# Moving weights read as two halves in turn, and the last modulation halves one chunk sooner

## Chip, cores and metric
The kernel runs on one core of one Trainium2 chip. The metric is the device time of one execution in microseconds, the median of several runs. All five engines of the core are in use: TensorE (PE; its weight loads are shown apart as PEld), VectorE (DVE), ScalarE (ACT), GpSimd (POOL) and SyncE (SP), whose queue issues nearly all loads.

## What is computed
Two transformer blocks over 256 tokens of width 2048, in float32, one after the other. Cut to its matmuls:

```python
# first block
a = rmsnorm(x);            proj = a @ w_in             # 2048 x 6662
mix = concat(hgrn2, forgetting attention, block attention)
h = x + mix @ w_out                                    # 2048 x 2048
c = rmsnorm(h)
h = h + (gelu(conv3(c @ w_gate)) * (c @ w_up)) @ w_down  # 2048 x 5632 twice, 5632 x 2048
h = h + sigmoid(rmsnorm(h) @ w_ple_gate) * (p @ w_ple_proj)
# second block
mod = silu(c_2) @ w_mod + b_mod                        # one row, 2048 x 12288: sh1 sc1 g1 sh2 sc2 g2
q, k, v, ... = (rmsnorm(x) * (1 + sc1) + sh1) @ w_in_2
x = x + g1 * (concat(window attention, latent attention) @ w_out_2)
u = relu((rmsnorm(x) * (1 + sc2) + sh2) @ w_ff1)       # 2048 x 8192
x = x + g2 * ((u * u) @ w_ff2)                         # 8192 x 2048
out = rmsnorm(x)
```

## The kernel before
Every large weight matrix is read from HBM once, in blocks of 128 partitions by 1024 float32 (two K-tiles of 512 columns, 512 KB), 757 of them. `prep` (L273 to 284) loads a block into a `raw` tile (4 buffers) and splits it: ScalarE writes `whi`, the value in float32r (L281), and VectorE writes `wlo`, the rest `raw - whi` (L282). Activations are split in the same way. A product of two float32 numbers is then three float32r matmuls: high by high, high by low, low by high.

There are two forms of the matrix product. In `linear` (L297 to 343) the activations (K-tile by 128 tokens) are the stationary operand and the weights, up to 512 columns, are the moving one. A block is 12 matmuls there: 2 halves of the tokens, 2 K-tiles, 3 products (L318 to 320). In `linear_t` (L346 to 365) 128 columns of the weights are stationary and the activations of all 256 tokens move: 24 matmuls a block (L360 to 362). `linear` does w_in, w_out, w_down, w_ple_gate, w_ple_proj, the second w_in and w_out, the first chunk of ff1 and all of ff2; `linear_t` does w_gate, w_up and ff1 chunks 1 to 15. Two small products inside the second attention (`expand`, L1287 and L1312) also have moving weights. Every matmul of `linear` and `linear_t` brings its own load of 128 stationary columns.

The host packs each matrix so that a block is one contiguous piece (`_pack`, L152). Weights are stored in their natural column order.

The order of the work is that of the program: after each block `tick()` runs what is due. A generator that is spawned yields a number of ticks after which its next part is placed, so that, for instance, a transpose is placed on TensorE's queue some blocks after its input was made. `tick()` also adds `mod_rate` to a counter and calls `mod_half()` for each whole one.

The modulation row is not made by TensorE. `mod_half()` (L910) loads half of 128 rows of the transposed w_mod (512 KB, tile `wmod`, 2 buffers), on SP's queue behind the latest weight load, and VectorE multiplies it with silu(c) and sums (L920). 192 halves make the whole row; the last 32 are done in `mlp2`, at one a tick from the end of ff1 chunk 0. `mod_upto(n)` does at once what is still missing. `mod_row` (L935) then adds the two halves and the bias (L931, L932), waits some ticks, transposes on TensorE (L940), copies on ScalarE (L942), and stores and reloads the row through HBM, so that it is on all partitions (L944, L947). The row made last is g2, which ff2 needs when it empties its accumulators (L1444).

`mlp2` runs ff1 chunks in four groups of four. After the first chunk of a group, ff2 runs on the group before: ff1 0 to 4, ff2 on 0 to 3, ff1 5 to 8, ff2 on 4 to 7, and so on. In the kernel before, `mod_upto(96)` and the g2 row come after ff1 chunk 4, right ahead of the first ff2:

```python
for g in range(4):
    for n in range(4):
        ff1(4 * g + n)
        ...
        if g == 1 and n == 0:
            self.mod_upto(96)
            self.spawn(self.mod_row([g2], 80, F))
        if n == 0 and pend is not None:
            ff2(pend, False)
```

Of the kernel before, what the change touches and what calls it, by code (L numbers as in the profile page):

```python
# [17 lines left out]
P = 128  # L18
# [3 lines left out]
CW = 512  # L22
NCH = D // CW
DFF = 5632
NF = DFF // CW
NF2 = 8192 // CW
# [122 lines left out]
    }  # L149


def _pack(w, widths, nk=2):  # L152
    k = w.shape[0]
    out = []
    c0 = 0
    for cw in widths:
        b = w[:, c0:c0 + cw].reshape(k // (nk * P), nk, P, cw).transpose(0, 2, 1, 3)
        out.append(np.ascontiguousarray(b).reshape(-1))
        c0 += cw
    return np.concatenate(out)  # L160


def layout(inputs):
    f = {k: np.asarray(v) for k, v in inputs.items()}
    sq = lambda n: f[n][0]
    x = f["x"][0]
    a = {}
    a["x"] = np.ascontiguousarray(x.reshape(2, P, D).transpose(1, 0, 2)).reshape(P, 2 * D)
    a["xT"] = np.ascontiguousarray(x.reshape(T, KT, P).transpose(2, 1, 0)).reshape(P, KT * T)
    pp = f["p"][0, 0]  # L170
    a["pT"] = np.ascontiguousarray(pp.reshape(T, 2, P).transpose(2, 1, 0)).reshape(P, 2 * T)
    a["gains"] = np.ascontiguousarray(np.concatenate(
        [f[n].reshape(c, P).T for n, c in GAINS], axis=1))
    w_in = sq("w_in")
    a["w_in"] = _pack(w_in[:, _w_in_cols()], [CW] * len(W_IN_CHUNKS))
    a["w_bf"] = np.ascontiguousarray(
        w_in[:, B_FG:B_FG + B_H].reshape(KT, P, B_H).transpose(1, 0, 2)).reshape(P, KT * B_H)
    a["w_out"] = _pack(sq("w_out"), [CW] * NCH)
    a["w_gate"] = _pack(sq("w_gate"), [CW] * NF)
    a["w_up"] = _pack(sq("w_up"), [CW] * NF)  # L180
    a["w_down"] = _pack(sq("w_down"), [CW] * NCH)
    a["w_pg"] = _pack(sq("w_ple_gate"), [CW] * NCH)
    a["w_pp"] = _pack(sq("w_ple_proj"), [CW] * NCH)
    a["w_mod"] = np.ascontiguousarray(sq("w_mod_2").T)
    a["w_in2"] = _pack(sq("w_in_2")[:, _w_in2_cols()], W_IN2_CHUNKS)
    uq = sq("w_uq_2").reshape(384, 8, 192)
    uqc = np.concatenate([uq[:, :4, :128].reshape(384, 512), uq[:, 4:, :128].reshape(384, 512),
                          uq[:, :, 128:].reshape(384, 512)], axis=1)
    a["w_uq"] = _pack(uqc, [CW] * 3, nk=3)
    ukv = sq("w_ukv_2").reshape(128, 8, 256)  # L190
    a["w_ukv"] = _pack(np.concatenate([ukv[:, :, :128].reshape(128, 1024),
                                       ukv[:, :, 128:].reshape(128, 1024)], axis=1),
                       [2 * CW] * 2, nk=1)
    a["w_out2"] = _pack(sq("w_out_2"), [CW] * NCH)
    a["w_ff1"] = _pack(sq("w_ff1_2"), [CW] * NF2)
    a["w_ff2"] = _pack(sq("w_ff2_2"), [CW] * NCH)
    a["fox_bf"] = f["fox_bf"].reshape(1, B_H)
    a["lb"] = f["lb_logits"].reshape(4, HD).T
    a["onorm"] = f["hgrn_onorm"].reshape(1, HD)
    a["c"] = f["c_2"].reshape(1, D)  # L200
    a["sinks"] = f["swa_sinks_2"].reshape(1, 16)
    a["rel"] = f["rel_bias_2"].reshape(32, 16)
    a["fing"] = f["final_norm_g_2"].reshape(1, D)
    a.update(shape_constants())
    return {k: np.ascontiguousarray(v) for k, v in a.items()}


def bc_rows(ap, n):
# [3 lines left out]
class K:  # L212
# [84 lines left out]
    def linear(self, xt, name, seq, off, cw, evac, before=None):  # L297


        nc = self.nc  # L300
# [6 lines left out]
        def products(c, b, i, w):  # L307
# [5 lines left out]
            o = ps[c][i][:, :cw]  # L313
            for j in range(2):
                xh, xl = xt(2 * b + j)
                wh = w[0][:, j * cw:(j + 1) * cw]
                wl = w[1][:, j * cw:(j + 1) * cw]
                nc.tensor.matmul(o, xh[:, sl], wh, start=st and j == 0, stop=False)  # L318
                nc.tensor.matmul(o, xh[:, sl], wl, start=False, stop=False)  # L319
                nc.tensor.matmul(o, xl[:, sl], wh, start=False, stop=en and j == 1)  # L320
# [611 lines left out]
        nc.vector.tensor_tensor(o, o, self.G("b_mod_2", k0, n), op=ALU.add)  # L932
        return o

    def mod_row(self, rows, k0, tmp):  # L935
        nc = self.nc
        col = self.mod_section(k0, 16)
        yield 2
        pt = self.aux()
        nc.tensor.transpose(pt[:16, :P], col, self.ident)  # L940
        rt = self.t(tmp, [P, 512], "t2", self.t2b)[:16, :P]
# [3 lines left out]
        n = D // len(rows)  # L945
# [174 lines left out]
    def mixer2(self, s):  # L1120
# [139 lines left out]
        def expand():  # L1260
# [18 lines left out]
            for i in range(2):  # L1279
# [3 lines left out]
                for kt in range(3):  # L1283
                    hi, lo = w2[kt]
                    xh, xl = cT[0][:, kt, sl], cT[1][:, kt, sl]
                    for l_, r_ in ((xh, hi), (xh, lo), (xl, hi)):
                        nc.tensor.matmul(pq, l_, r_, start=(k == 0), stop=(k == 8))  # L1287
                        k += 1
                do_rope(qr[i].rearrange("p (h d) -> p h d", h=8), pq.rearrange("p (h d) -> p h d", h=8), i, 8)
            yield 1  # L1290
# [15 lines left out]
            for i in range(2):  # L1306
                sl = slice(i * P, (i + 1) * P)
                for n in range(2):
                    ws = slice(n * CW, (n + 1) * CW)
                    pq = self.aux()  # L1310
                    for k, (l_, r_) in enumerate(((ch[:, sl], hi), (ch[:, sl], lo), (cl[:, sl], hi))):
                        nc.tensor.matmul(pq, l_, r_[:, ws], start=(k == 0), stop=(k == 2))  # L1312
                    nc.scalar.activation(vb[:, i, 4 * n:4 * n + 4, :].rearrange("p h d -> p (h d)"), pq, AF.Copy)
            yield 3
            for h in range(8):
# [54 lines left out]
    def out_proj2(self):  # L1370
        nc, M = self.nc, self.M
        g1 = self.g1
        self.spawn(self.mod_row(g1, 32, M))
        ss = self.t(self.C, [P, 2, 4], "ss", 2)

        def evac(c, i, ps):
# [25 lines left out]
    def mlp2(self):  # L1402
        nc = self.nc
        with ExitStack() as s:
# [64 lines left out]
            pend = None  # L1469
            for g in range(4):  # L1470
                for n in range(4):
                    ff1(4 * g + n)
                    if g == 0 and n == 0:
                        self.holdctx.close()
# [1 line left out]
                        self.mod_open(None)  # L1476
                        g2 = self.t(R, [P, D], "grow")
                        self.mod_rate = 1.0
                    if g == 1 and n == 0:
                        self.mod_upto(96)  # L1480
                        self.spawn(self.mod_row([g2], 80, F))
                    if n == 0 and pend is not None:
                        ff2(pend, False)
                pend = list(range(4 * g, 4 * g + 4))
# [30 lines left out]
```

## Time and profile before

| | us |
|---|---|
| median of 3 runs | 2290.66 (2286.03 to 2298.77) |
| the profiled execution | 2293.44 |
| its span, first to last instruction | 2291.7 |
| TensorE busy | 2246.7 |
| VectorE busy | 1573.5 |
| ScalarE busy | 1105.6 |

The mean granted TensorE clock is 0.993 of full speed. In the span's order of time: w_in, the first attention and w_out (to 467.8 us), w_gate and w_up with w_down in three groups (to 1201.8), the gate of the per-layer input and the head of the second w_in (to 1324.7), the rest of the second attention and w_out_2 (to 1548.4), ff1 and ff2 (to the end). DMA moves 226 GB/s on average. Matmuls are pipelined, so a row's duration overlaps with the next; the spacing of two starts is the pace.

### The profile page before, as it was taken

How to read it: one execution, taken by the hardware profiler on the slowest of the kernel's cores; microseconds unless marked ns; L12 is line 12 of the kernel's file. 1: busy time of each engine (PE TensorE's matmuls, PEld its weight loads, DVE VectorE, ACT ScalarE, POOL GpSimd, SP SyncE). 2: the span in 40 equal slices, each digit the busy share in tenths (PEclk: the TensorE clock that was granted, in tenths of full speed). 3: DMA queues.
4: the chain of work that ended last, by engine and by line, in shares of the span. 5: the costliest groups of instructions: out<-in, count | busy, mean ns of one | idle time of the engine just before them, and what ended most of it. 6: DMA issues, size and time to landing. Idle time of an engine off the chain costs nothing.

```text
span 2291.7 us, 34932 instructions
## 1 busy us (share of the span) xinstructions
PE 2246.7 (98%) x13714; PEld 1996.9 (87%) x13714; DVE 1573.5 (69%) x2329; ACT 1105.6 (48%) x1560; POOL 25.8 (1%) x35
## 2 busy tenths in 40 slices
PE   9999999999999999999999999999999999999998
PEld 7787887899998999989987788888878998998986
DVE  6777766777876677767777866768766555555555
ACT  6655554454444444434445655655433443443444
POOL 0000000000000000000000000000000000000000
PEclk9999999999999999999999999999999999999999
DMA  8665566677777777777778643566886566656554
GB/s 300 229 211 193 205 230 208 241 254 259 265 264 261 265 252 254 256 258 264 249 255 301 241 161 117 173 194 212 309 290 193 190 187 193 190 187 193 190 188 154
DMA packets 147537, 517.82 MB, mean 226 GB/s; under 512 B 17115, under 2 KB 21292, under 8 KB 146860
## 3 DMA queue, kind: packets, MB, share of 16 engines
q1 hardware_dynamic: 147228, 515.58, 66.3%
q8 instruction: 107, 1.75, 0.3%
q14 instruction: 58, 0.48, 0.1%
q10 hardware_dynamic: 144, 0.01, 0.0%
HBM read 513.38 MB, written 2.14 MB: 225 GB/s over the span
## 4 chain that ended last, share of the span: by engine, by line
PE 80%; DMA 7%; issue 6%; DVE 5%; ACT 1%; POOL 1%; SPq 0%; DVEq 0%; ACTq 0%; POOLq 0%
PE mm L320 14%; PE mm L319 14%; PE mm L318 14%; PE mm L362 11%; PE mm L361 11%; PE mm L360 11%; DMA wmod<-in_w_mod 6%; DVE wlo L282 2%; PE aux L382 1%; DVE wmod L920 1%; PE aux L750 1%; ACT whi L281 1%; DMA raw<-in_w_ff 0%; PE aux L824 0%; PE aux L1273 0%
## 5 line engine op out<-in xcount | busy, mean ns | idle before, releaser
L281 ACT ACTIVATE whi<-raw 128x1024 fp32r<-128x1024 f32 (+1 forms) x746 | 785.9, 1055 | 999.0 <-PE mm L320 539.9
L282 DVE TENSOR_TENSOR wlo<-raw,whi 128x1024 fp32r<-128x1024 f32 (+1 forms) x746 | 905.5, 1216 | 503.6 <-ACT whi L281 501.9
L362 PE MATMUL mm<-xt,wlo 128*128 128x256 f32 x2368 | 662.6, 280 | 5.8 <-DVE wlo L282 5.8
L361 PE MATMUL mm<-xt,whi 128*128 128x256 f32 x2368 | 661.5, 279 | 0.0
L360 PE MATMUL mm<-xt,whi 128*128 128x256 f32 x2368 | 661.5, 279 | 0.0
L361 PEld LDWEIGHTS mm<-xt,whi 128*128 128x128 f32 x2368 | 451.0, 190 | 0.3
L362 PEld LDWEIGHTS mm<-xt,wlo 128*128 128x128 f32 x2368 | 444.6, 188 | 7.4 <-DVE wlo L282 7.2
L360 PEld LDWEIGHTS mm<-xt,whi 128*128 128x128 f32 x2368 | 444.6, 188 | 0.3
L319 PE MATMUL mm<-wlo,hid 128*128 128x512 f32 x848 | 331.4, 391 | 1.0 <-DVE wlo L282 1.0
L318 PE MATMUL mm<-whi,hid 128*128 128x512 f32 x848 | 331.6, 391 | 0.0
L320 PE MATMUL mm<-whi,hid 128*128 128x512 f32 x848 | 331.2, 391 | 0.0
L920 DVE SCALAR_TENSOR_TENSOR wmod<-wmod,cact 128x1024 f32<-128x1024 f32 x192 | 234.5, 1221 | 109.3 <-DMA wmod<-in_w_mod 108.5
L318 PE MATMUL mm<-whi,xt 128*128 128x512 f32 (+2 forms) x660 | 260.3, 395 | 0.9 <-ACT whi L281 0.9
L319 PE MATMUL mm<-wlo,xt 128*128 128x512 f32 (+2 forms) x660 | 256.9, 389 | 3.5 <-DVE wlo L282 3.5
L320 PE MATMUL mm<-whi,xt 128*128 128x512 f32 (+2 forms) x660 | 256.3, 389 | 0.0
L319 PEld LDWEIGHTS mm<-wlo,hid 128*128 128x128 f32 x848 | 159.9, 189 | 35.1 <-DVE wlo L282 2.3
L318 PEld LDWEIGHTS mm<-whi,hid 128*128 128x128 f32 x848 | 159.9, 189 | 33.0
L320 PEld LDWEIGHTS mm<-whi,hid 128*128 128x128 f32 x848 | 159.8, 188 | 33.1
L319 PEld LDWEIGHTS mm<-wlo,xt 128*128 128x128 f32 x660 | 124.5, 189 | 29.3 <-DVE wlo L282 6.6
L318 PEld LDWEIGHTS mm<-whi,xt 128*128 128x128 f32 x660 | 124.3, 188 | 24.6 <-ACT whi L281 1.6
L320 PEld LDWEIGHTS mm<-whi,xt 128*128 128x128 f32 x660 | 124.4, 188 | 23.7
L318 PE MATMUL mm<-whi,mix 128*128 128x512 f32 x244 | 97.9, 403 | 0.0
(349 smaller groups left out, 1796.6 us busy)
## 6 DMA issues: line engine op xcount, KB each, us to landing
raw<-in_w_ff SPq DMA_DIRECT2D x256, 512.0 KB, 3.7
wmod<-in_w_mod SPq DMA_DIRECT2D x192, 512.0 KB, 5.0
raw<-in_w_in SPq DMA_DIRECT2D x120, 512.0 KB, 4.1
raw<-in_w_gate SPq DMA_DIRECT2D x88, 512.0 KB, 3.8
raw<-in_w_up SPq DMA_DIRECT2D x88, 512.0 KB, 4.2
raw<-in_w_down SPq DMA_DIRECT2D x88, 512.0 KB, 4.0
raw<-in_w_out SPq DMA_DIRECT2D x64, 512.0 KB, 3.8
raw<-in_w_pg SPq DMA_DIRECT2D x32, 512.0 KB, 4.6
```

What stands on the lines that cost most here:

```text
L281: nc.scalar.activation(hi[:, :ncol], raw[:, :ncol], AF.Copy)
L282: nc.vector.tensor_tensor(lo[:, :ncol], raw[:, :ncol], hi[:, :ncol].bitcast(F32), op=ALU.subtract)
L318: nc.tensor.matmul(o, xh[:, sl], wh, start=st and j == 0, stop=False)
L319: nc.tensor.matmul(o, xh[:, sl], wl, start=False, stop=False)
L320: nc.tensor.matmul(o, xl[:, sl], wh, start=False, stop=en and j == 1)
L360: nc.tensor.matmul(o, hi[:, ws], xh, start=first, stop=False, skip_group_check=True)
L361: nc.tensor.matmul(o, hi[:, ws], xl, start=False, stop=False, skip_group_check=True)
L362: nc.tensor.matmul(o, lo[:, ws], xh, start=False, stop=(b == last and j == 1), skip_group_check=True)
L382: self.nc.tensor.transpose(pt[:, j * P:(j + 1) * P], src[:, j * P:(j + 1) * P], self.ident)
L750: nc.tensor.transpose(pt[:, jo * P:(jo + 1) * P], L[:, j * P:(j + 1) * P], self.ident)
L920: nc.vector.scalar_tensor_tensor(raw, raw, 1.0, self.cact[:, us], op0=ALU.mult, op1=ALU.mult, accum_out=self.macc[:, j, u:u + 1])
```

## The change
Three edits.

The packing. Each chunk of columns of a weight matrix that is a moving operand is stored with its even columns first and its odd columns behind them. Chunks that serve as stationary operand (`turn`) keep their order. The value part of w_ukv, 1024 columns, keeps its place and size and is permuted within each of its two runs of 512.

The reading. `moving(w)` turns a slice of 2n columns into the pattern (n, 2): column 0 of the first half, column 0 of the second, column 1 of the first, and so on. TensorE thus reads the columns in their natural order from two places half a chunk apart (1024 bytes for 512 columns), and writes its output as before. Stationary operands, the splits and the loads are as they were.

The modulation. `mod_upto(96)` and the g2 row stand ahead of ff1 chunk 4, and the row's transpose is placed 5 ticks later instead of 2. The other use of `mod_row` keeps 2.

```diff
-def _pack(w, widths, nk=2):
+def _pack(w, widths, nk=2, turn=()):
...
-    for cw in widths:
-        b = w[:, c0:c0 + cw].reshape(k // (nk * P), nk, P, cw).transpose(0, 2, 1, 3)
+    for n, cw in enumerate(widths):
+        b = w[:, c0:c0 + cw]
+        if n not in turn:
+            b = np.concatenate([b[:, 0::2], b[:, 1::2]], axis=1)
+        b = b.reshape(k // (nk * P), nk, P, cw).transpose(0, 2, 1, 3)
...
-    a["w_gate"] = _pack(sq("w_gate"), [CW] * NF)
-    a["w_up"] = _pack(sq("w_up"), [CW] * NF)
+    a["w_gate"] = _pack(sq("w_gate"), [CW] * NF, turn=range(NF))
+    a["w_up"] = _pack(sq("w_up"), [CW] * NF, turn=range(NF))
...
-    a["w_ff1"] = _pack(sq("w_ff1_2"), [CW] * NF2)
+    a["w_ff1"] = _pack(sq("w_ff1_2"), [CW] * NF2, turn=range(1, NF2))
...
+def moving(w):
+    return w.rearrange("p (a b) -> p b a", a=2)
...
-                wh = w[0][:, j * cw:(j + 1) * cw]
-                wl = w[1][:, j * cw:(j + 1) * cw]
+                wh = moving(w[0][:, j * cw:(j + 1) * cw])
+                wl = moving(w[1][:, j * cw:(j + 1) * cw])
...
-    def mod_row(self, rows, k0, tmp):
+    def mod_row(self, rows, k0, tmp, wait):
...
-        yield 2
+        yield wait
...
                 for n in range(4):
+                    if g == 1 and n == 0:
+                        self.mod_upto(96)
+                        self.spawn(self.mod_row([g2], 80, F, 5))
                     ff1(4 * g + n)
...
-                    if g == 1 and n == 0:
-                        self.mod_upto(96)
-                        self.spawn(self.mod_row([g2], 80, F))
                     if n == 0 and pend is not None:
```

## Rows read from the trace of the kernel before

**Rows 1.** The page, busy time of each engine: us (share of the span) xinstructions.
```profile
PE 2246.7 (98%) x13714; PEld 1996.9 (87%) x13714; DVE 1573.5 (69%) x2329; ACT 1105.6 (48%) x1560; POOL 25.8 (1%) x35
```

**Rows 2.** Groups by form: instruction, tiles, shape, count, busy us, mean ns, idle before.
```profile
L282 DVE TENSOR_TENSOR wlo<-raw,whi 128x1024 fp32r<-128x1024 f32 x727 | 887.3, 1223 | 492.4 <-ACT whi L281 490.7
L362 PE MATMUL mm<-xt,wlo 128*128 128x256 f32 x2368 | 662.6, 280 | 5.8 <-DVE wlo L282 5.8
```

**Rows 3.** Timeline of PE (start us, duration us), ff2: matmuls 1 and 54.
```profile
2099.79 0.39 PE L318 MATMUL mm<-whi,hid 128*128 128x512 f32 x1
...
2111.80 0.39 PE L320 MATMUL mm<-whi,hid 128*128 128x512 f32 x1
```

**Rows 4.** Timeline of PE, 384-wide chunk: matmuls 1 and 8.
```profile
1423.83 0.33 PE L318 MATMUL mm<-whi,xt 128*128 128x384 f32 x1
...
1425.04 0.33 PE L319 MATMUL mm<-wlo,xt 128*128 128x384 f32 x1
```

**Rows 5.** Timeline of PE, bf16 warm-up: its last three matmuls.
```profile
4.98 0.38 PE L492 MATMUL aux<-junk 128*128 128x512 bf16 x1
5.20 0.38 PE L492 MATMUL aux<-junk 128*128 128x512 bf16 x1
5.41 0.38 PE L492 MATMUL aux<-junk 128*128 128x512 bf16 x1
```

**Rows 6.** Timeline of PE, first w_in block: two neighbours.
```profile
9.12 0.63 PE L318 MATMUL mm<-whi,xt 128*128 128x512 f32 x1
9.55 0.63 PE L319 MATMUL mm<-wlo,xt 128*128 128x512 f32 x1
```

**Rows 7.** Timeline of PE, latent attention, plain float32: two neighbours.
```profile
1425.39 0.38 PE L1254 MATMUL aux<-PT,vb 128*128 128x256 f32 x1
1425.61 0.38 PE L1254 MATMUL aux<-PT,vb 128*128 128x256 f32 x1
```

**Rows 8.** Timeline of PE, L1287: matmuls 2 and 17 of 18.
```profile
1360.13 0.40 PE L1287 MATMUL aux<-wlo,cT 128*128 128x512 f32 x1
...
1363.63 0.39 PE L1287 MATMUL aux<-wlo,cT 128*128 128x512 f32 x1
```

**Rows 9.** Timeline of PE, linear_t in w_gate: matmuls 1 and 55.
```profile
499.79 0.28 PE L362 MATMUL mm<-xt,wlo 128*128 128x256 f32 x1
...
505.91 0.28 PE L362 MATMUL mm<-xt,wlo 128*128 128x256 f32 x1
```

**Rows 10.** Windows: length, busy us (x) by engine, granted clock, DMA share, GB/s.
```profile
4.98:5.63 0.65, 0.65 (x4) 0.20 (x2) 0.04 (x1) 0.57 (x2) 0.00 (x0) 1.00 1.13 403
8.70:9.90 1.20, 1.20 (x4) 0.99 (x3) 1.20 (x3) 0.52 (x1) 0.00 (x0) 0.50 1.07 393
...
40.00:467.80 427.80, 415.15 (x1991) 343.29 (x1991) 308.78 (x582) 228.16 (x415) 17.28 (x19) 0.99 0.63 219
...
775.30:956.10 180.80, 180.80 (x1536) 180.77 (x1535) 135.12 (x175) 82.76 (x90) 0.00 (x0) 1.00 0.73 255
...
1214.50:1324.70 110.20, 106.12 (x473) 84.76 (x472) 86.44 (x125) 61.36 (x87) 2.52 (x4) 1.00 0.72 253
...
1579.10:1676.30 97.20, 91.38 (x776) 89.53 (x775) 75.80 (x99) 42.20 (x48) 0.00 (x0) 1.00 0.88 307
1676.50:1771.70 95.20, 90.62 (x386) 73.41 (x385) 57.29 (x66) 35.64 (x36) 0.00 (x0) 0.96 0.71 237
```

**Rows 11.** Timeline of PE, first ff2: around the transpose of the g2 row.
```profile
1698.48 0.40 PE L320 MATMUL mm<-whi,hid 128*128 128x512 f32 x1
1702.50 0.38 PE L940 MATMUL aux<-ident,modT 128*16 128x128 f32 x1 [3.62 <-DVE modT L932]
...
1703.96 0.63 PE L318 MATMUL mm<-whi,hid 128*128 128x512 f32 x1
...
1707.80 0.57 PE L318 MATMUL mm<-whi,hid 128*128 128x512 f32 x1
```

**Rows 12.** Timeline of DVE, first ff2: the last half.
```profile
1700.80 1.23 DVE L920 SCALAR_TENSOR_TENSOR wmod<-wmod,cact 128x1024 f32<-128x1024 f32 x1 [2.27 <-DMA wmod<-in_w_mod]
```

More of the change, by code (lines that the diff above doesn't have):

```diff
@@ L188, in layout @@
                           uq[:, :, 128:].reshape(384, 512)], axis=1)
-    a["w_uq"] = _pack(uqc, [CW] * 3, nk=3)
+    a["w_uq"] = _pack(uqc, [CW] * 3, nk=3, turn=(0, 1))
     ukv = sq("w_ukv_2").reshape(128, 8, 256)
-    a["w_ukv"] = _pack(np.concatenate([ukv[:, :, :128].reshape(128, 1024),
-                                       ukv[:, :, 128:].reshape(128, 1024)], axis=1),
-                       [2 * CW] * 2, nk=1)
+    a["w_ukv"] = np.concatenate([_pack(ukv[:, :, :128].reshape(128, 1024), [2 * CW], nk=1, turn=(0,)),
+                                 _pack(np.concatenate(np.split(ukv[:, :, 128:].reshape(128, 1024), 2, axis=1)),
+                                       [CW])])
     a["w_out2"] = _pack(sq("w_out_2"), [CW] * NCH)
-    a["w_ff1"] = _pack(sq("w_ff1_2"), [CW] * NF2)
+    a["w_ff1"] = _pack(sq("w_ff1_2"), [CW] * NF2, turn=range(1, NF2))
     a["w_ff2"] = _pack(sq("w_ff2_2"), [CW] * NCH)
@@ L1286, in expand @@
                     for l_, r_ in ((xh, hi), (xh, lo), (xl, hi)):
-                        nc.tensor.matmul(pq, l_, r_, start=(k == 0), stop=(k == 8))
+                        nc.tensor.matmul(pq, l_, moving(r_), start=(k == 0), stop=(k == 8))
                         k += 1
@@ L1311, in expand @@
                     for k, (l_, r_) in enumerate(((ch[:, sl], hi), (ch[:, sl], lo), (cl[:, sl], hi))):
-                        nc.tensor.matmul(pq, l_, r_[:, ws], start=(k == 0), stop=(k == 2))
+                        nc.tensor.matmul(pq, l_, moving(r_[:, ws]), start=(k == 0), stop=(k == 2))
                     nc.scalar.activation(vb[:, i, 4 * n:4 * n + 4, :].rearrange("p h d -> p (h d)"), pq, AF.Copy)
@@ L1372, in out_proj2 @@
         g1 = self.g1
-        self.spawn(self.mod_row(g1, 32, M))
+        self.spawn(self.mod_row(g1, 32, M, 2))
         ss = self.t(self.C, [P, 2, 4], "ss", 2)
```

## The prediction
> **What bounds the kernel now.** I read the busy line first: TensorE is busy 98% of 2291.7 us [rows 1]. That share does not say how close the stream is to its best, so I read the groups by form next [rows 2], and then the spacing of single matmuls in the timeline, start to start. The program gives the counts: a 512-wide chunk of K = 2048 is 8 blocks of 2 K-tiles, each with 2 token halves and 3 products, 12 matmuls a block. Blocks that go through linear at width 512: 13 w_in chunks (104), out_proj1 (32), w_down (88), w_pp (4), w_pg (32), two w_in2 chunks (16), out_proj2 (32), ff1 chunk 0 (8), ff2 (128): 444 blocks, 5328 matmuls. One w_in2 chunk is 448 wide and one 384 wide: 96 matmuls each. linear_t has 7104 matmuls of 256 columns (three lines of 2368 [rows 2]).
>
> In ff2, 53 steps take 2111.80 - 2099.79 = 12.01 us: 226.6 ns for 512 columns [rows 3]. At 2.4 GHz 512 columns are 213.3 ns, so 13.3 ns, 32 cycles, are not columns. Four readings say what kind of thing that is.
> - At 384 columns 7 steps take 1.21 us, 173 ns against 160: again 13 ns, though the stream is a quarter shorter [rows 4].
> - The bf16 warm-up matmuls, also 512 wide and at granted clock 1.00, stand 0.21 to 0.22 us apart [rows 5, 10]. I take 216 ns, the figure between the two.
> - The same float32r product at granted clock 0.50 takes 0.43 us a step; 512 columns at 1.2 GHz are 426.7 ns, no excess [rows 6, 10].
> - Plain float32, 256 columns in 0.22 us, is two cycles a column, with 2 to 3 ns over [rows 7].
>
> So the excess appears only where 4 bytes per partition are read in each 2.4 GHz cycle, and is per matmul (that is, per 128-column weight load) rather than per column. It also moves with place and phase: L1287, whose stationary operand is another tile, needs (1363.63 - 1360.13) / 15 = 233 ns for 512 columns [rows 8]; the 256-column stream of linear_t runs at 6.12 us / 54 = 113.3 ns in one stretch [rows 9] and at 180.8 us / 1536 = 117.7 ns in another, with the same operands [rows 10]. I read it as two SBUF reads, the moving stream and the weight load behind it, meeting now and then; order of addresses can alter that.
>
> **The change part by part.** *Two halves in turn.* No instruction, byte or DMA is added: the packing is on the host, split writes the same tiles, output columns arrive in their old order. What changes is the address of each successive moving column: neighbours become words half a chunk apart, and each half advances one word per two cycles. No row of the trace has a moving operand read this way. Bounds from rows: 216 ns from below (the bf16 stream of the same width at the same clock, [rows 5]), two cycles a column, 427 ns, from above (the plain float32 stream, [rows 7]; it reads in order, but is the slowest warm stream there is). I take 216, the end that the present 226.6 lies nearest to: three of four stream kinds have no more than that floor, and the fourth has an excess that shifts with address and phase.
>
> The sum: 5328 x (226.7 - 216) = 57.0 us; 96 x (173 - 163) + 96 x about 13 (taken as the 384 chunk's excess) = 2.2 us. Together 59.2 us if every nanosecond reaches the end. Where it does not:
> - First stages to 467.8 us: 1632 matmuls, 17.4 us. TensorE idles 12.65 us of 427.8 there [rows 10], the attention chains and the start behind loads; a shorter stream uncovers more of that. I keep 80%: -3.5.
> - w_pg with its prefetch: 384 matmuls, 4.1 us; TensorE busy 106.1 of 110.2 from 1214.5 to 1324.7 [rows 10]. I keep half: -2.1.
> - Second attention (w_in2, out_proj2), 2.0 + 2.2 + 4.1 = 8.3 us: I keep 85%: -1.3.
> - First ff2 group, 384 matmuls, 4.1 us, still behind loads at its head: -1.1.
> - w_down and the later ff2 groups: kept whole. A block would last 12 x 216 = 2.59 us, and DVE needs 1.22 us per block for wlo [rows 2], ACT less.
> That leaves 51 us. If the cover were gone everywhere but in w_down and ff2 (1056 + 1536 matmuls, less 1.1 us), 27 us would be left.
>
> [...]
>
> *linear_t* keeps its order (its chunks are excluded from the packing), so its 7104 matmuls cost what they did, unless the phase in which they start changes (a rival).
>
> *Last modulation halves.* mod_upto(96) now stands ahead of ff1(4). By the ticks 24 of the last 32 halves are due by then; so 8 halves, each a 512 KB load on SP and a DVE product of 1.23 us [rows 12] with its accumulator read, go ahead of that chunk instead of beside its 8 blocks, and with them two small DVE adds, the transpose on PE, a copy on ACT, and the store and broadcast load on SP, past ff1(4)'s 8 weight loads. The transpose comes 5 ticks later instead of 2. Now it stands some 22 us into ff2 (begun at 1676.5) and stalls the queue: 1698.48 to 1702.50, 3.8 us beyond a step, and what is queued behind it, the matmuls of ff2, then runs at half clock to 1707.80, about 12 x 0.2 = 2.5 us more [rows 11]. The whole group takes 95.2 us against 384 x 0.2267 = 87.0: 8.2 us to be had [rows 10]. Against it: ff1(1) to ff1(4), 97.2 us for 768 x 0.1133 = 87.0, already waits for loads at DMA share 0.88 and 307 GB/s [rows 10]. A 0.52 MB load costs 1.7 us at that rate, and some four halves that land in ff2 today would have to land inside this stage: +6.8 us, and the wmod tile has only two buffers. The queue order is not shown, so the ends are -8 and +8; I take -2.
>
> Total -53 us. From the profiled execution's 2293.4 us that gives 2240.4; the median of the runs shown is 2.8 us below that execution, so 2238 us.
>
> **Rivals.**
> - *linear_t locks into its shorter spacing.* Five groups, 1536 + 768 + 768 + 768 + 576 = 4416 matmuls, run at 117.7 ns (the row is of the first), all entered from linear; conv_ffn's first group runs at 113.3. A linear of another spacing may hand over in the other phase. 4416 x 4.4 = 19.5 us more: 2218 us. For it: same operands, two spacings [rows 9, 10]. Against: nothing in linear_t is edited.
> - *Half the excess goes*, or half of the gain drowns in waits: 26 + 2 us, 2263 us. For it: 233 and 226.6 ns show that the excess has levels, not just presence.
> - *Order does not matter.* The weight load still takes its 13 ns: only the -2 us are left, 2289 us. For it: the excess is the same at 384 and 512 columns. [...]
> - *Slower: each column starts a new read.* If what SBUF hands over at once serves several neighbouring columns, an order that leaves the place at every column needs a read per column. Place: every linear block. Price: up to 5328 x 200 = 1066 us, about 3355 us; at L1287's spacing 5328 x 6.6 = 35 us, about 2324. It decides from 229.2 ns a step on (13.5 us / 5328 = 2.5 ns over today). For it: in-order streams are all that the trace has. Against: excess already varies without any change of order.
> [...]
>
> **How the numbers follow.** Forecast 0.42, shorter linear_t 0.20, half 0.15, no effect 0.09, slower 0.14. A measurement of this kernel can tell about 0.5%, 11.5 us, from no change; so faster 0.77, same 0.09, slower 0.14. The forecast's own range is 2224 (all 59 us kept, modulation -8) to 2272 (cover gone, 27 us, modulation +8). The range for 8 in 10 reaches from the sum of all gains, 2290.7 - 59 - 8 - 19.5 = 2204, to no effect with a little on top, 2292; the slower case stays out.
>
> **What would show it.** In ff2 and w_down the spacing of L318 to L320: 216 ns right, 226.7 no effect, anything above 229 the slower rival. linear_t at 117.7 or 113.3 in 775 to 956. The 448 and 384 chunks by the same 10 ns or so. The transpose L940's counterpart with no 4 us gap before it and no stretch at clock 0.50; if instead waits of PE for wlo grow in ff1(4), the moved halves cost what they gave. The prediction is wrong if linear's spacing is right and the time is not below 2265, for then the cover was misjudged.

## The result, and the profile after

| | before | after |
|---|---|---|
| median, us | 2290.44 (2286.03 to 2298.77) | 2238.05 (2235.57 to 2238.65) |
| span of the profiled execution, us | 2291.7 | 2236.4 |
| TensorE busy, us | 2246.7 | 2172.8 |

The ratio is 0.9765 with a 95% interval of 0.9736 to 0.9794. The forecast said 2238. That the number is met to the microsecond is luck: the gain in `linear` came out some 8 us smaller than forecast, and `linear_t`, put at nothing, gave some 15 us. Lines have moved by 10: L318 to L320 are now L328 to L330, L360 to L362 are L370 to L372, L282 is L292, L920 is L930, L932 is L942, L940 is L950.

The page's busy line after (columns as in [rows 1]; the granted clock is 0.993, as before):

```profile
PE 2172.8 (97%) x13714; PEld 1986.3 (89%) x13714; DVE 1569.8 (70%) x2329; ACT 1104.9 (49%) x1560; POOL 25.8 (1%) x35
```

The same 13714 matmuls, 73.9 us less of them, and a share that fell from 98% to 97%: part of what the stream gave back turned into idle time. PE's timeline in ff2, two matmuls 53 steps apart (start us, duration us; the counterpart of [rows 3]), then two of the 384-wide chunk, 7 steps apart ([rows 4]):

```profile
1839.86 0.38 PE L328 MATMUL mm<-whi,hid 128*128 128x512 f32 x1
...
1851.30 0.38 PE L330 MATMUL mm<-whi,hid 128*128 128x512 f32 x1
...
1385.06 0.33 PE L329 MATMUL mm<-wlo,xt 128*128 128x384 f32 x1
...
1386.20 0.33 PE L330 MATMUL mm<-whi,xt 128*128 128x384 f32 x1
```

11.44 us over 53 is 215.8 ns where it was 226.6; 1.14 over 7 is 163 where it was 173. What a column takes, two widths read in turn show: e5 (below) has 215.8 ns for 512 columns and 135.8 for 320, so 192 columns take 80.0 ns, 0.4167 ns each, the pace that the prediction writes as a column a cycle at 2.4 GHz. A cycle below stands for these 0.4167 ns. 512 columns are then 213.3 ns and 384 are 160.0, and the excess over them fell from 13.3 ns to 2.5 and from 13 to 3. Now linear_t, which was not edited: two matmuls 54 steps apart in w_gate's second group, and behind those the windows of after (columns as in [rows 10]).

```profile
769.78 0.28 PE L371 MATMUL mm<-xt,whi 128*128 128x256 f32 x1
...
775.90 0.28 PE L371 MATMUL mm<-xt,whi 128*128 128x256 f32 x1
```
```profile
40.00:455.60 415.60, 398.59 (x1987) 343.21 (x1986) 307.24 (x580) 226.97 (x414) 17.28 (x19) 0.99 0.65 225
...
760.10:934.60 174.50, 174.42 (x1538) 174.20 (x1537) 136.00 (x177) 83.05 (x90) 0.00 (x0) 1.00 0.75 264
1183.90:1304.00 120.10, 111.85 (x516) 94.74 (x516) 90.22 (x130) 65.08 (x94) 2.54 (x4) 0.99 0.71 247
1541.90:1641.50 99.60, 91.74 (x777) 89.17 (x776) 75.93 (x98) 41.82 (x47) 0.00 (x0) 1.00 0.87 300
1641.50:1735.20 93.70, 86.11 (x387) 73.19 (x386) 57.98 (x66) 36.11 (x37) 0.00 (x0) 0.98 0.72 241
1735.30:1822.40 87.10, 87.10 (x770) 87.08 (x769) 49.01 (x49) 41.04 (x45) 0.00 (x0) 1.00 0.61 195
1905.30:1995.70 90.40, 90.40 (x769) 90.40 (x768) 49.02 (x49) 40.87 (x45) 0.00 (x0) 1.00 0.60 189
```

6.12 us over 54 is 113.3 ns; the same group took 117.7 before (180.80 us for 1536 in [rows 10], 174.50 now). Read the last two windows side by side: the same code on the same shapes, 768 matmuls each, one at 113.4 and one at 117.7. Four of the five groups that ran at 117.7 have the short spacing after the change, one (1905.3) has not.

Stage by stage, before to after, in us of span (one profiled execution each; stages cut at the first matmul of each product):

| stage | before | after | difference |
|---|---|---|---|
| w_in, first attention, w_out | 461.1 | 448.9 | -12.2 |
| w_gate and w_up, three groups | 220.5 + 180.9 + 90.5 | 221.6 + 174.5 + 87.1 | -8.7 |
| w_down (and w_pp), three groups | 87.0 + 87.1 + 80.7 | 82.9 + 83.9 + 78.3 | -9.7 |
| w_pg and the head of w_in_2 | 119.9 | 120.1 | +0.2 |
| second attention, w_out_2, ff1 chunk 0 | | | -6.8 |
| ff1 chunks 1 to 4 | 97.4 | 99.6 | +2.2 |
| first ff2 | 95.4 | 93.8 | -1.6 |
| ff1 chunks 5 to 15, three groups | 90.5 + 90.4 + 67.8 | 87.1 + 90.4 + 65.3 | -5.9 |
| ff2, other groups, and the end | 87.1 + 87.1 + 96.9 | 82.9 + 82.9 + 92.5 | -12.8 |
| all | 2291.7 | 2236.4 | -55.3 |

Not every row of this table repeats. The programs of the experiments run the same code in some stages. With linear in order (before, e2, e3, e5, e6) the first stage took 451.0 to 461.2 us and w_pg 119.9 to 123.2; with linear in turn (after, e1, e4) they took 443.4 to 448.9 and 120.0 to 121.3. On the means the first stage thus gains 9 us and w_pg 1. In the four of the in-order programs that also leave the halves alone, ff1 chunks 1 to 4 took 97.4 to 99.7 and the first ff2 93.4 to 96.0. The groups of ff1 chunks 5 to 15 and the later ff2 repeat to 0.1 us where the spacing is the same.

Last, the transpose of the g2 row in the first ff2, in PE's timeline (the counterpart of [rows 11]):

```profile
1665.68 0.38 PE L330 MATMUL mm<-whi,hid 128*128 128x512 f32 x1
1670.06 0.28 PE L950 MATMUL aux<-ident,modT 128*16 128x128 f32 x1 [4.00 <-DVE modT L942]
...
1671.47 0.63 PE L329 MATMUL mm<-wlo,hid 128*128 128x512 f32 x1
```

The stall is still there (4.00 us of waiting, 3.62 before), 28.6 us into ff2 where it was 26.0, and so is the stretch at half clock behind it (granted clock 0.50 from 1671.5 to 1674.0 us, 0.43 us a step). The modulation edit did not move what it was meant to move.

### The profile page after: what moved, and what is told of

It is laid out like the page before. It is cut to its first block, busy times and chain, and to the rows that moved or that the text cites. A ratio compares the mean times of both kernels' runs of the same rounds, so it can differ in the third digit from the quotient of the medians.

```text
span 2236.4 us, 34936 instructions
## 1 busy us (share of the span) xinstructions
PE 2172.8 (97%) x13714; PEld 1986.3 (89%) x13714; DVE 1569.8 (70%) x2329; ACT 1104.9 (49%) x1560; POOL 25.8 (1%) x35
## 4 chain that ended last, share of the span: by engine, by line
PE 73%; DMA 11%; DVE 7%; issue 6%; ACT 2%; POOL 1%; SPq 0%; DVEq 0%; POOLq 0%; ACTq 0%
PE mm L330 12%; PE mm L329 12%; PE mm L328 12%; PE mm L372 11%; PE mm L371 11%; PE mm L370 11%; DMA wmod<-in_w_mod 9%; DVE wlo L292 4%; DVE wmod L930 1%; PE aux L392 1%; ACT whi L291 1%; PE aux L760 1%; DMA raw<-in_w_ff 0%; SPq L288 0%; PE aux L1283 0%
## 5 line engine op out<-in xcount | busy, mean ns | idle before, releaser
L292 DVE TENSOR_TENSOR wlo<-raw,whi 128x1024 fp32r<-128x1024 f32 (+1 forms) x746 | 903.8, 1216 | 410.2 <-ACT whi L291 408.9
L372 PE MATMUL mm<-xt,wlo 128*128 128x256 f32 x2368 | 656.6, 277 | 6.6 <-DVE wlo L292 6.6
L370 PE MATMUL mm<-xt,whi 128*128 128x256 f32 x2368 | 655.2, 277 | 0.0
L372 PEld LDWEIGHTS mm<-xt,wlo 128*128 128x128 f32 x2368 | 444.5, 188 | 9.1 <-DVE wlo L292 8.8
L370 PEld LDWEIGHTS mm<-xt,whi 128*128 128x128 f32 x2368 | 445.7, 188 | 0.2
L930 DVE SCALAR_TENSOR_TENSOR wmod<-wmod,cact 128x1024 f32<-128x1024 f32 x192 | 234.8, 1223 | 156.2 <-DMA wmod<-in_w_mod 155.5
L329 PE MATMUL mm<-wlo,hid 128*128 128x512 f32 x848 | 322.7, 381 | 4.1 <-DVE wlo L292 4.0
L328 PE MATMUL mm<-whi,hid 128*128 128x512 f32 x848 | 322.4, 380 | 0.0
L330 PE MATMUL mm<-whi,hid 128*128 128x512 f32 x848 | 322.4, 380 | 0.0
L329 PE MATMUL mm<-wlo,xt 128*128 128x512 f32 (+2 forms) x660 | 250.8, 380 | 6.2 <-DVE wlo L292 6.0
L328 PE MATMUL mm<-whi,xt 128*128 128x512 f32 (+2 forms) x660 | 253.3, 385 | 0.9 <-ACT whi L291 0.9
L330 PE MATMUL mm<-whi,xt 128*128 128x512 f32 (+2 forms) x660 | 249.3, 378 | 0.0
L328 PEld LDWEIGHTS mm<-whi,hid 128*128 128x128 f32 x848 | 160.7, 190 | 22.6
L330 PEld LDWEIGHTS mm<-whi,hid 128*128 128x128 f32 x848 | 160.6, 189 | 22.7
L328 PEld LDWEIGHTS mm<-whi,xt 128*128 128x128 f32 x660 | 125.2, 190 | 17.4 <-ACT whi L291 1.7
L330 PEld LDWEIGHTS mm<-whi,xt 128*128 128x128 f32 x660 | 125.3, 190 | 15.5
L329 PE MATMUL mm<-wlo,mix 128*128 128x512 f32 x244 | 93.1, 382 | 2.3 <-DVE wlo L292 2.3
```

The lines of the kernel that those rows point to most:

```text
L292: nc.vector.tensor_tensor(lo[:, :ncol], raw[:, :ncol], hi[:, :ncol].bitcast(F32), op=ALU.subtract)
L370: nc.tensor.matmul(o, hi[:, ws], xh, start=first, stop=False, skip_group_check=True)
L372: nc.tensor.matmul(o, lo[:, ws], xh, start=False, stop=(b == last and j == 1), skip_group_check=True)
L930: nc.vector.scalar_tensor_tensor(raw, raw, 1.0, self.cact[:, us], op0=ALU.mult, op1=ALU.mult, accum_out=self.macc[:, j, u:u + 1])
```

## The experiments

| run | median us (lowest to highest, runs) | ratio to before, 95% interval |
|---|---|---|
| e1_order_only | 2245.14 (2239.97 to 2248.19, 5) | 0.9803, 0.9778 to 0.9829 |
| e2_halves_only | 2290.80 (2283.76 to 2298.60, 12) | 0.9999, 0.9982 to 1.0016 |
| e4_tokens_in_turn | 2222.37 (2214.86 to 2224.12, 4) | 0.9699, 0.9672 to 0.9725 |
| e7_early_halves | 2227.71 (2221.06 to 2232.05, 4) | 0.9721, 0.9696 to 0.9746 |
| e8_turn_and_early | 2210.75 (2208.15 to 2217.81, 5) | 0.9652, 0.9628 to 0.9677 |
| e9_all_halves_early | 2209.68 (2198.04 to 2215.99, 6) | 0.9625, 0.9592 to 0.9658 |

The kernel before had medians of 2287.99, 2288.76 and 2296.49 beside them (e1 to e4, e5 to e8, e9). e3, e5 and e6 were run once, for their traces.

**The two halves of the change apart.** e1 is the kernel after with the modulation edit taken back:

```diff
-                    if g == 1 and n == 0:
-                        self.mod_upto(96)
-                        self.spawn(self.mod_row([g2], 80, F, 5))
                     ff1(4 * g + n)
...
+                    if g == 1 and n == 0:
+                        self.mod_upto(96)
+                        self.spawn(self.mod_row([g2], 80, F, 2))
```

> The reading in turn alone: packing and moving() as changed, the modulation halves back behind ff1 chunk 4 with 2 ticks. Theory (the order of the moving reads is the whole gain, the moved halves give nothing): linear at 215.8 ns a step as in the changed kernel, and a time within 6 us of its 2238. Rival 1 (the moved halves cost what ff1(1..4) and the first ff2 lost, 2.2 + 2.5 us): about 2233. Rival 2 (the moved halves give 2 us or more): 2240 to 2246. linear_t may start its groups at either spacing in any kernel; each group of 768 at the other spacing is 3.4 us.

e2 is the kernel before with that edit alone.

> The moved halves alone: kernel before with mod_upto(96) and the g2 row ahead of ff1 chunk 4 and 5 ticks, weights in their old order. Theory: the order on SP, PE and POOL comes out as before, so the same stall of 4 us before the g2 transpose and the same time, 2290 +- 5; linear at 226.7 ns a step. Rival 1 (the prediction's -2 to -8): 2282 to 2288 and a gap before the transpose under 1 us. Rival 2 (halves crowd ff1(1..4)): 2295.

Measured: e1 has linear at 215.8 ns everywhere and 2245.1 us, e2 has it at 226.7 ns and 2290.8. The edit of the modulation gives nothing that shows by itself (its interval reaches from 4 us less to 4 us more, so 2 us either way can't be told), and the order is the gain. The time of e1 alone misses its theory by 1 us and lies in rival 2's range, 7 us above the kernel after; the two intervals overlap a little. In the traces it isn't the halves that cost e1 its time: its first ff2 was shorter than that of the kernel after, 89.9 us against 93.8, and what was longer is its first w_gate group, which nothing in either edit touches, 229.7 us against 221.7, most of it at 117.7 ns. The wait before the transpose goes with neither edit: 3.6 us before, 4.0 after, 2.8 in e1, 2.5 in e2.

**Why the edit of the halves does nothing.** The last 32 halves on DVE, in both kernels (count, duration in ns, then first and last start), before and after:

```profile
L920 DVE SCALAR_TENSOR_TENSOR wmod<-wmod,cact x32: 1211/1225/1226, 1579.8 to 1700.8; 128x1024 f32<-128x1024 f32 x32
```
```profile
L930 DVE SCALAR_TENSOR_TENSOR wmod<-wmod,cact x32: 1214/1225/1229, 1544.0 to 1668.4; 128x1024 f32<-128x1024 f32 x32
...
  DMA wmod<-in_w_mod: 33.2, 27
```

They take 121.0 us before and 124.4 after, one in about 4 us, and in the kernel after DVE waited for the transfer of 27 of the 32 (last line: us in all, times). Asking for eight of them a chunk sooner leaves the two `wmod` buffers and the loads behind the same weight loads as before: the rows of SP, PE and POOL stand in one and the same order in both programs.

**What the order does.** e3 is the kernel before with 48 matmuls of each of 16 forms at its end, which differ in how the moving tile is read:

```diff
+forms = [("pOrder", 512, P, same), ("pTurn", 512, P, turn(2)), ("pQuarter", 512, P, turn(4)), ...
+         ("pPair", 512, P, runs(2)), ("pStepB", 512, P, step(2)), ... ("pHalfSt", 512, 64, same), ...
+         ("pShort", 256, P, same), ("pShortTurn", 256, P, turn(2)), ("pTiny", 128, P, same), ...
```

> Kernel before with 768 extra matmuls behind its end, 48 of each form, float32r, with the activations' and weights' tile shapes of linear; the result is untouched. Steps in ns. In order 512 columns: 226.7; two halves in turn: 216. Theory A (the moving stream collides with the weight load because it walks through addresses twice as fast as the load; in turn both walk alike): quarters and eighths in turn walk slower than the load and collide again, over 216; pairs of columns in turn walk alike: 216; every second column walks four times as fast: over 216; a stationary operand of 64 or 32 columns in order: excess 1/2 and 1/4 of 10.9 ns, so about 221 and 218.5; 256 columns in order 113.3 or 117.7, in turn 109. [...]

PE's timeline of it, for each form two matmuls 30 steps apart:

```profile
2291.20 0.39 PE L519 MATMUL pOrder<-pmv,pst 128*128 128x512 f32 x1
2298.03 0.39 PE L519 MATMUL pOrder<-pmv,pst 128*128 128x512 f32 x1
...
2302.07 0.38 PE L519 MATMUL pTurn<-pmv,pst 128*128 128x512 f32 x1
2308.55 0.38 PE L519 MATMUL pTurn<-pmv,pst 128*128 128x512 f32 x1
...
2312.61 0.45 PE L519 MATMUL pQuarter<-pmv,pst 128*128 128x512 f32 x1
2321.11 0.45 PE L519 MATMUL pQuarter<-pmv,pst 128*128 128x512 f32 x1
...
2349.73 0.51 PE L519 MATMUL pPair<-pmv,pst 128*128 128x512 f32 x1
2359.58 0.51 PE L519 MATMUL pPair<-pmv,pst 128*128 128x512 f32 x1
...
2377.87 0.63 PE L519 MATMUL pStepB<-pmv,pst 128*128 128x512 f32 x1
2391.40 0.63 PE L519 MATMUL pStepB<-pmv,pst 128*128 128x512 f32 x1
...
2441.71 0.39 PE L519 MATMUL pHalfSt<-pmv,pst 128*64 128x512 f32 x1
2448.61 0.39 PE L519 MATMUL pHalfSt<-pmv,pst 128*64 128x512 f32 x1
```

In order 6.83 / 30 = 228 ns here (227 over the whole form), halves in turn 216. In the other forms quarters in turn take 283, eighths 487, two columns of each half in turn 328, every second column 451, every fourth 461, every eighth 431. Four columns of each half in turn take 246 to 254. So it is not true that any order other than the plain one escapes the excess: nearly all are worse, up to 487 ns, 0.95 ns a column. The reading that a weight load behind the matmul collides with the stream (theory A) is not borne out either: a load of 64 stationary columns instead of 128 (pHalfSt) leaves 230 ns and one of 32 leaves 232, where it asked for about 221 and 218.5, and pairs take 328 where it asked for 216. At 256 columns the plain order needs 120 ns, again 13 ns over the 106.7 of its columns, and turn 111.7; and 128 columns take 111.7 in either order, so about 111.7 ns is the least a float32r matmul with 128 stationary columns took here.

e5 varies the two streams: how far apart they are, how long each run is before the next pair of runs, where the tile starts, and bfloat16.

```diff
+("pApart257", 512, even, streams(2, 256, 257)), ... ("pApart512", 512, even, streams(2, 256, 512)),
+("pBlock128", 512, even, blocks(128)), ... ("pBlock4", 512, even, blocks(4)),
+("pFourFar", 512, even, streams(4, 128, 256)), ("pFourOff", 512, even, streams(4, 128, 132)),
+("pWide448", 448, even, order(448)), ... ("pBfOrder", ...), ("pBfTurn", halves), ("pBfStep", evens)
```

> The kernel before with extra matmuls at its end whose results are not used, 36 of each form, all with a 128-wide stationary tile unless said; only their steps are read. The earlier probe gave 226.7 ns in order and 215.8 in two halves in turn at 512 columns, 119.9 in order at 256: an excess of 32 cycles of 2.4 GHz (13.3 ns) over one column a cycle at both widths. Theory F, a fixed excess of each matmul that is read in order: pWide448 200 ns and pWide320 146.7 ns. Theory G, an excess with each so many columns: 198 and 141.7. Distance of the two streams (pApartN: columns apart, pTurn is 256): theory D1, any two streams that are far apart are free, all of pApart257 to pApart512 at 215.8; theory D2, the distance must be a multiple of 1 KB: pApart512 215.8 and the others between 226.7 and 328 (the pairs in turn of the earlier probe). pBlockN (two neighbouring runs of N columns in turn, then the next two): theory D1 215.8 down to some width and towards 328 below it (pBlock4 at 250 or more); theory D2 all of them 226.7 or worse. pFourFar and pFourOff (four streams, 256 and 132 columns apart; 128 apart gave 283): if four streams are too many 283 in both, if it was their distance 216 in one of them. pStStep (stationary tile every second column, moving in order): if the stationary tile's own read matters, other than 226.7; pStTurn with the moving tile in turn 215.8. pBfOrder, pBfTurn, pBfStep (bfloat16): no excess to take away, 213 to 216 in the first two; no number for the step.

PE's timeline of it: streams 257 columns apart, runs of 4, and four streams, each as two matmuls 30 steps apart:

```profile
2327.68 0.38 PE L535 MATMUL pApart<-pmv,pst 128*128 128x512 f32 x1
2334.15 0.38 PE L535 MATMUL pApart<-pmv,pst 128*128 128x512 f32 x1
...
2436.27 0.38 PE L537 MATMUL pBlock<-pmv,pst 128*128 128x512 f32 x1
2442.74 0.38 PE L537 MATMUL pBlock<-pmv,pst 128*128 128x512 f32 x1
...
2454.88 0.44 PE L536 MATMUL pFourOff<-pmv,pst 128*128 128x512 f32 x1
2463.04 0.44 PE L536 MATMUL pFourOff<-pmv,pst 128*128 128x512 f32 x1
```

The distance does not matter here: two streams 257, 260, 264, 272, 288, 320, 384 or 512 columns apart all stand at 215.8 ns (258 at 216.6), and runs of 128, 64, 32, 16, 8 and 4 columns too, where the two streams are 16 bytes apart. Theory D1 held further down than it claimed, D2 fell. Four streams are too many at any distance tried (283 and 272). What is shown is narrow: strictly one column of each of two streams, in turn, runs at 215.8; plain order, more streams and longer runs of each do not. In plain order the excess came in several sizes: 320 columns 146.7 ns (32 cycles over, as theory F has it), 448 columns 206.6 (48 cycles, which neither theory has), 512 columns from a start 2 columns on 233.3 (48), from 4 columns on 231.7. In turn nothing of that is seen: 189.1 ns at 448 columns and 135.8 at 320. A stationary tile that takes every second column makes 233.3 in order, where the same stream has 227.7 with the plain tile (pAgain), and 215.8 in turn, so how the stationary operand lies does have a part in the plain order's excess, though not by the width that theory A went by. Why two in turn are free is not settled by these runs.

bfloat16 behaves the other way round, against the expectation (three groups of 36, start and length; the granted clock was 1.00 in all):

```profile
2512.37 7.94 PE L544 MATMUL pBfOrder<-junk 128*128 128x512 bf16 x36
2520.15 17.60 PE L544 MATMUL pBfTurn<-junk 128*128 128x512 bf16 x36
2537.59 8.29 PE L544 MATMUL pBfStep<-junk 128*128 128x512 bf16 x36
```

From start to start, in order 7.78 / 36 = 216 ns, halves in turn 17.44 / 36 = 484, every second column 226 by its own steps.

**linear_t's two spacings.** e4 is the kernel after with the tokens, linear_t's moving operand, read in turn as well; the accumulators then hold its tokens in another order, and what empties them puts them back:

```diff
                     xh, xl = xt(2 * b + j)
+                    xh, xl = moving(xh), moving(xl)
...
-                    evac(m // 2, ps[m // 2].rearrange("p (j t) -> p j t", j=2))
+                    evac(m // 2, ps[m // 2].rearrange("p (j u i) -> p j i u", j=2, i=2))
```

> The changed kernel, and linear_t too reads its moving operand in turn: the two halves of the tokens, one token of each; its accumulators then hold the tokens in that order and are read back with stride 2 when emptied. Theory A (collision of the moving stream with the weight load, 16 to 27 cycles in 256 columns): 109 ns a step in all linear_t groups in place of 113.3 or 117.7; (1920 + 3648) x 4.3 + 768 x 8.7 = 31 us less, and nothing in ff1 chunks 1 to 4, which wait for loads: about 2207. Rival 1 (a floor of 16 cycles per 256 columns that order does not touch): 113.3 in all groups, about 2235. Rival 2 (emptying with stride 2 is slower and shows): 2240 or more, with VectorE's and ScalarE's operations on the accumulators longer than 0.68 and 0.59 us.

PE's timeline of it, 54 steps apart in w_gate's second group:

```profile
799.76 0.28 PE L377 MATMUL mm<-xt,whi 128*128 128x256 f32 x1
...
805.79 0.28 PE L377 MATMUL mm<-xt,whi 128*128 128x256 f32 x1
```

6.03 / 54 = 111.7 ns, the least of the probe, in this and every other group: between theory A's 109 and rival 1's 113.3. 2222.4 us: 0.9699 of before, 15.7 us under the kernel after by the medians, and the intervals are apart. Rival 2 is out: VectorE's and ScalarE's operations that empty the accumulators kept their 0.68 and 0.59 us.

e6 asks what chooses between 113.3 and 117.7 where the tokens are read in order:

```diff
+        if name != "w_up" and off // (D * CW) in (5, 9, 13):
+            nc.tensor.matmul(self.aux()[:, :P], xt(0)[0][:, :P], xt(0)[0][:, P:], start=True, stop=True)
```

> The kernel before with one matmul of 128 columns more (its result is not used) at the start of linear_t's chunks 5 and 9 of w_gate and 5, 9 and 13 of w_ff1, nothing else. Theory P (a phase taken at the hand-over from the 512-wide steps and kept until the next stall sets linear_t's spacing): with another matmul between them the groups of w_gate at 775 us and 1043 us and of w_ff1 at 1772, 1950 and 2127 us, all at 117.8 ns in the kernel before, change in some or all cases to 113.3; each that changes saves 4.4 ns a matmul (768: 3.4 us, 1536: 6.8 us), five of them about 19 us. Rival Q (the spacing belongs to what the group reads and where its tiles lie): all stay at 117.8, time within 3 us of before.

PE's timeline where the group begins, with the matmul put in (L353):

```profile
765.29 0.22 PE L353 MATMUL aux<-xt 128*128 128x128 f32 x1
...
765.52 0.28 PE L363 MATMUL mm<-xt,whi 128*128 128x256 f32 x1
...
771.41 0.28 PE L362 MATMUL mm<-xt,whi 128*128 128x256 f32 x1
```

The last two rows are 50 steps apart, 117.8 ns. All five groups stayed at 117.8 to 117.9, 2286.4 us: no support for theory P from this disturbance. Rival Q does not hold either, because the spacing of one and the same group differs between programs: the third w_gate group has 113.3 after and 117.8 in e7, and the first has 113.3 before and after and mostly 117.7 in e1 and e2. That first group shows more, because it changes inside one program. PE's timeline of it in e1, two matmuls 48 steps apart, then a wait, then two matmuls 48 steps apart:

```profile
458.88 0.28 PE L370 MATMUL mm<-xt,whi 128*128 128x256 f32 x1
...
464.32 0.28 PE L370 MATMUL mm<-xt,whi 128*128 128x256 f32 x1
...
465.89 0.67 PE L969 MATMUL aux<-t,ones 128*128 128x256 f32 x2 [0.60 <-DVE t L967]
...
466.63 0.28 PE L370 MATMUL mm<-xt,whi 128*128 128x256 f32 x1
...
472.28 0.28 PE L370 MATMUL mm<-xt,whi 128*128 128x256 f32 x1
```

5.44 / 48 is 113.3 ns ahead of the wait, 5.65 / 48 is 117.7 behind it, and so it stays to the end of the group. The kernels before and after have a wait in the same place and keep 113.3 behind it. In ff1 chunks 1 to 4, which wait often, the spacing changes both ways, and in the eight traces with linear_t in order it never changes within a stretch without a wait (a step of over 125 ns), a stretch's first few steps aside. So the half of theory P that says a spacing is kept until the next stall holds. The link to linear's pace shows in the counts: the five groups that the prediction's rival names had 117.8 in all five programs with linear in order, 25 of 25, and in the three with linear in turn (after, e1, e7) in 4 of 15 cases. What picks the spacing at a given stall stays open; that reading in turn ends the choice is shown.

**Where w_pg's gain went.** The waits of PE in w_pg's stage, before and after (us in total, times, longest):

```profile
PE aux L382 <- DVE hn L1101: 2.4, 1, 2.4
PE mm L319 <- DVE wlo L282: 1.4, 2, 1.1
```
```profile
PE aux L392 <- DVE hn L1111: 5.2, 2, 4.1
PE mm L329 <- DVE wlo L292: 3.0, 4, 1.7
```

3.8 us became 8.2, about the 4.1 us that the shorter stream gave there. All are on VectorE, which in the kernel after is busy 90.22 us of the 120.10. At 0.36 a step, the last 18 of the first 160 modulation halves (the expectation below counts 17) are done in a bunch, about 4 us apart, at the end of the first block, 15 of them in this stage, and the kernel before has the same bunch there. e7 issues them a little sooner, all the way from the start:

```diff
-                    self.mod_rate = 0.36
+                    self.mod_rate = 0.41
```

> The kernel after with the modulation halves issued a little faster from the first stage on (0.41 a step in place of 0.36), so that the 17 halves that were bunched at the end of the first block, 15 of them in w_pg's stage, are done before it. Theory V (w_pg's gain was eaten by VectorE, which does 15 halves of 1.3 us there beside the splitting of the weights and the norm): w_pg's stage falls from 120.1 us to 112 to 116, the earlier stages take the halves within their slack, total about 2232. Rival W (w_pg waits for the evictions and the norm, not for VectorE's halves): 119 to 121, total within 3 us of after. Rival X (the halves cost in the earlier stages what w_pg gains, through DMA and the splitting): w_pg 112 to 116, total within 3 us of after.

The window and the waits of that stage in e7:

```profile
1179.00:1294.90 115.90, 109.93 (x515) 95.38 (x514) 73.27 (x95) 65.36 (x94) 2.53 (x4) 0.99 0.60 190
```
```profile
PE aux L392 <- DVE hn L1111: 6.0, 2, 4.9
```

115.9 us, at the upper end of theory V: the waits for wlo are gone, the wait for the norm's `hn` is not. e8 and e9 below repeat it with 116.3 and 115.4. What is left is a wait on the chain of accumulators, norm and transpose; a kernel that shortens that chain was not run. In the median e7 is 10 us under after, of which this stage is 4; the two intervals overlap, so the sum is less certain than the stage.

e8 puts e4 and e7 together.

> The kernel after with linear_t's tokens read in turn as well (2222.4 us in its earlier run) and the modulation halves at 0.41 a step. Theory V: 2216 to 2218; rivals W and X: 2220 to 2224.

2210.8 us, 0.9652 of before: below all the ranges expected, theory V's 2216 too, about what the gains of e4 (15.7) and e7 (10.3) make together, and lower than both kernels of the case.

**All halves early.** The stage that the modulation edit was aimed at still loses: in e8, ff1 chunks 1 to 4 take 99.0 us and the first ff2 89.9. e9 does all 192 halves before w_pg:

```diff
-                    self.mod_rate = 0.41
+                    self.mod_rate = 0.49
...
-            self.mod_upto(80)
+            self.mod_upto(96)
...
-                        self.mod_open(None)
                         g2 = self.t(R, [P, D], "grow")
-                        self.mod_rate = 1.0
+                        self.spawn(self.mod_row([g2], 80, F, 2))
```

> As the run with tokens in turn and 0.41 halves a step (2210.8 us), but with all 192 modulation halves before w_pg (0.49 a step from the first stage on), so that none is left beside ff1 and the first ff2, and the last gate's row is made in ff1's chunk 1. Theory V (the halves cost where VectorE and the transfers are short of time, in ff1's chunks 1 to 4 and the first ff2, and little before): ff1(1 to 4) falls from 99.0 us to 86 to 88 (768 steps of 111.7 ns are 85.8), the first ff2 from 89.9 to 83 to 85, the earlier stages lose up to 8 us to 32 halves more: total 2196 to 2206. Rival X (a half costs the same wherever it lies, 32 x 1.3 us on VectorE and 16 MB of transfers): the same two stages fall, but the stages to w_pg grow by 15 us or more, total 2208 to 2220.

The two stages in e9 (windows):

```profile
1548.60:1635.70 87.10, 87.01 (x779) 86.82 (x778) 49.15 (x49) 42.51 (x49) 0.00 (x0) 1.00 0.66 207
1635.70:1718.60 82.90, 82.90 (x387) 72.60 (x386) 48.36 (x49) 35.40 (x35) 0.00 (x0) 1.00 0.64 202
```

They run almost without a gap now, 18.9 us shorter, and at full clock. But w_pg begins at 1196.1 us, where it began at 1173.9 in e8: 22.2 us later, spread over all stages before it (the first 8.2, the three groups of w_gate to w_down 14 together). By the stages this is rival X: theory V allowed 8 us there. The 8.2 us of the first stage are less sure than the 14, because that stage differs by 10 us between traces of the same code. The medians, 2209.7 and 2210.8 us, can't decide it: the kernel before stood at 2296.5 beside the one and at 2288.8 beside the other, and the two intervals overlap. A half thus costs TensorE some 0.6 us beside ff1 and ff2 (18.9 / 32) and 0.4 to 0.7 (14 / 32, 22.2 / 32) ahead of w_pg, an estimate from one trace of each program. That 17 halves moved forward in e7 cost the earlier stages nothing that shows, and 32 more did, says where their slack ends.

## Why the prediction was right, step by step

- *Linear's pace, 226.7 to 216 ns:* right, 215.8 in every group, and 163 at 384 columns. The bound taken from the bf16 stream of the same width [rows 5] was the right one; the probe's own bf16 rows in order (216) confirm it. That the order reaches this bound was a choice of the nearer end, not worked out, and bfloat16 in the same order takes 484.
- *What of it reaches the end, 51 us:* too much. By the table it was 42.9 (the stages of linear: -12.2, -9.7, +0.2, -6.8, -1.6, -12.8). Mis-sized was the cover: w_pg, where half of 4.1 us was to be kept, kept nothing (0 to 1 us by the other traces, and e7 takes 4.2 us off by undoing VectorE's bunch of halves); the first stages lost 5.2 of 17.4 where 3.5 were put down, and by the means of the other traces 8; w_down with w_pp lost some 2 where nothing was put down, part of it in waits for VectorE (in the last two of its groups 1.9 us, 0.5 before). In the stages where TensorE idled before [rows 10], it idled longer after: 17.0 us against 12.65 from 40 us to the end of the first stages.
- *linear_t unchanged:* this step failed. 1536 + 768 + 768 + 576 matmuls took 4.3 ns less each, 15.7 us. It is the rival with a chance of 0.20, which came for four of its five groups while the likeliest case's main term fell short by 8. That the spacing is locked, and that it goes with the pace of the linear before, is borne out by the traces (25 of 25 against 4 of 15). How the hand-over picks it is not shown: e6 put a matmul there and nothing changed, and in e1 and e2 the first group lost the short spacing at a wait inside it.
- *Last modulation halves, -2:* the step did not happen. The prediction said that the queue order is not shown; it did not change: SyncE's rows stand in the old order. The halves arrive as transfers allow, in 124.4 us, and the transpose stalls as it did [rows 11]; e2 measures 0.9999. ff1 chunks 1 to 4 became 2.2 us longer; e1 has 99.5 us and e2 96.6, but e6, with neither edit, has 99.7, so what made them longer is not shown.
- *The reading of the excess* as two reads that meet, the stream's and the weight load's, is not supported as it was put: narrower loads leave it (230 and 232 ns). That the stationary operand has some part is not out (233.3 ns with every second column). What makes the excess stays open. That half the excess goes, or that order does not matter, is out by the 215.8 ns.
- *Slower, each column a new read:* wrong for this change, but its neighbours are slower: had the halves been quarters, 283 ns a step would have meant 5328 x 56 = 300 us more (an estimate from the probe). So the risk that it priced was a real one, though no run shows a read for each column as its cause. How far a column lies from the one before does not sort e3's forms: 4 bytes (in order) take 227 ns, 8 bytes (every second column) 451, and 1024 bytes (halves in turn) 215.8.

So -42.9, -14.6 (linear_t without ff1 chunks 1 to 4) and +2.2 make -55.3 of span, against -51, 0 and -2. The medians differ by 52. The forecast is met because 15 us of a rival filled what cover and the halves had taken: that the order takes the excess of linear away was right, though its reason is not shown, and the agreement of the sum is luck.

## What to carry to other kernels

Measure the spacing of matmuls start to start against what the columns alone take, as two widths show it (0.4167 ns each here): the excess, 13.3 ns of 226.6, was the hint here that the way the operand is read could be changed. For float32r, in these runs, a moving operand read as two streams, one column of each in turn, took it away, at every distance of the two that was tried (4 to 512 columns) and with no instruction more, because the host packs. Do not generalise that order to four or eight streams, to pairs or to bfloat16, where it took 1.2 to 2.2 times the plain step; measure the one form at the end of the kernel first. Before you trust a difference of one stage, look how far that stage repeats in programs that do not change it. And when TensorE's stream is made shorter, look at once for work on another engine that bunches in a stage (here 15 halves in one stage): spreading it out gave back what the shorter stream had lost there, but moving all of it only moved its cost.

## What was not expected of the hardware

- Two float32r streams in turn run at 215.8 ns for 512 columns even when they are 16 bytes apart (runs of 4), while two columns of each in turn take 328.
- The same order doubles a bfloat16 matmul, 216 to 484 ns; every second column costs bfloat16 only 226, and float32r 451.
- The plain order's excess comes in sizes (32, 44 or 48 cycles of 0.4167 ns in e5's forms, 16 or about 27 in linear_t) and depends on the tile's start (from 2 columns on 233.3 ns); linear_t in unchanged code runs at 113.3 or 117.7 ns, kept the one it had through hundreds of matmuls and changed it only at a wait in the eight traces with it in order.
- About 111.7 ns was the least step of a float32r stream with 128 stationary columns, at 128 and at 256 moving ones alike.
